# Two layers of a diffusion block and two of a second block on one core: column sums of the norms in sets of four tiles, and the scalings and biases around the norms on other engines

## The chip, the cores and the metric

One core of a Trainium2 chip runs the kernel. The metric is the time of one execution on the device in microseconds; three executions of the kernel before were timed. Engines are TensorE (PE, its weight loads PEld), VectorE (DVE), ScalarE (ACT), GpSimd (POOL) and SyncE (SP, which issues the DMAs).

## What is computed

The reference, cut to what matters here. All is float32, D is 1024, 512 latent tokens and, in layer 0, 256 context tokens.

```python
def layer_norm(t, g, b):
    tf = t.astype(jnp.float32)
    mu = jnp.mean(tf, axis=-1, keepdims=True)
    var = jnp.mean(jnp.square(tf - mu), axis=-1, keepdims=True)
    return ((tf - mu) * lax.rsqrt(var + LN_EPS)).astype(t.dtype) * g + b

def conformer_conv(u, dw_w, dw_b, ln_g, ln_b, pw_w, pw_b):
    a, gt = jnp.split(u, 2, axis=-1)
    h = depthwise_conv(a * jax.nn.sigmoid(gt), dw_w, dw_b)
    h = jax.nn.silu(layer_norm(h, ln_g, ln_b))
    return h @ pw_w + pw_b

def first_block(...):
    for l in range(DEPTH):
        ...
        attn_l = latent_attention(q_l, k_l, v_l, k_c, v_c)
        x = layer_norm(DEEPNORM_ALPHA * x + ml[..., 2, :] * mix(zl, attn_l), ln1_g[l], ln1_b[l])
        x = layer_norm(DEEPNORM_ALPHA * x + ml[..., 5, :] * ffn(modulate(x, ml[..., 3, :], ml[..., 4, :])),
                       ln2_g[l], ln2_b[l])
        ...
    return x

def second_block(x, p, positions, ...):
    h = x
    for i in range(DEPTH):
        u = rmsnorm(h, ln_mix[i]) @ w_in[i]
        ...
        h = h + jnp.concatenate([y_mla, y_gla], axis=-1) @ w_out[i]
        gate = jax.nn.sigmoid(rmsnorm(h, ple_norm[i]) @ w_ple_gate[i])
        h = h + gate * (p[i] @ w_ple_proj[i])
    return rmsnorm(h, final_norm)
```

`mix` adds three gated branches (attention, the conv branch above, a pooling branch) and multiplies by `w_out`. In layer 0 the context tokens go the same way with modulations of their own; in layer 1 only the latent tokens leave the block.

## The kernel before

Activations lie feature-major: a tensor of 1024 features is eight tiles of 128 partitions, with tokens along the free axis (768 in layer 0, 512 in layer 1 and in the second block). A product in float32 is three matmuls: operands are split into a high and a low part, and `proj` issues hi x hi, lo x hi and hi x lo. Weights come by DMA into `wr`; ScalarE casts the high part (`wh`, L178), VectorE subtracts the low one (`wl`, L181). All matmuls are issued from one line, L186.

A layer norm works on the eight tiles. `ln_center` (L231) adds the columns of each tile with a matmul against ones (`colsum`, L221): the sum of tile i goes to 32 columns of TensorE and 32 partitions of a PSUM tile `st`, column tile i % 4, so that tiles 0 and 4 share one. A matmul against `cmean` then adds the four parts and broadcasts, and VectorE subtracts the mean (L243). `inv_rms` (L246) squares each tile on ScalarE (L252) and issues that tile's sum right behind its square:

```python
        for i, y in enumerate(ys):
            sq = tmp()
            nc.scalar.activation(sq[:, :n], y, AF.Square)
            j = i % 4
            ...
                self.mm(s2[32 * j:32 * j + 32, c:c + w], self.ones[:, :32], sq[:, c:c + w], i < 4, i >= m - 4)
```

The reciprocal root is a chain of small VectorE steps (L209 to L214), and `ln_tile` broadcasts it over the partitions with identity matmuls. `ln_split` (L278) scales a tile on VectorE (L281), adds the bias and rounds to the high part on ScalarE (L282), and takes the low part on VectorE (L283); `split` does the last two for other tiles (L286, L287). In a chunk of over 512 tokens a sum is two matmuls.

A layer of the first block runs `mixer`, then `out_ffn`:
- at the end of `mixer` the conv norm: eight tiles reloaded from DRAM (L719), its sums between the projections of the gates, then for each tile scale (VectorE, L732), bias (GpSimd, L733), tanh (ScalarE, L735), product (VectorE, L736) and split; then the pointwise projection `conv_pw`, whose results are gated and added to the other branches (L750, L751) and split for `w_out`;
- in `out_ffn` the eight tiles of x are loaded (L778) and multiplied by ALPHA plus a bias on GpSimd (L780); the output projection adds into them on VectorE (L795); LN1 follows in two sections of tokens (512 and 256 in layer 0, 256 and 256 in layer 1), its scale copied to a tile `rs` (L800), `ln_split` gives the FFN's input, and GpSimd scales the raw tiles for the residual (L808, L809), with `ag` the gain and bias times ALPHA;
- the FFN adds into the same tiles (L831), and LN2's sums follow.

Between the layers `ln_split` makes layer 1's input from LN2, and GpSimd scales the tiles again (L1005, L1006) and stores them to DRAM tiles `xd`, which layer 1 loads as x. Behind layer 1 every second tile's bias is added on GpSimd (L1023). The second block's norms are RMS norms (`inv_rms` alone, tiles `pt`).

The order on each engine is set by a scheduler that simulates the program with a cost model, so the text of the program gives dependencies and a first order only. Each engine then runs its instructions in that fixed order.

Of the kernel before, what the change touches and what calls it, by code (L numbers as in the profile page):

```python
# [20 lines left out]
P = 128  # L21
D = 1024
KT = 8
# [54 lines left out]
class Net:  # L78
# [106 lines left out]
    def mm(self, out, l, r, start, stop):  # L185
        self.nc.tensor.matmul(out, l, r, start=start, stop=stop)  # L186
# [35 lines left out]
    def colsum(self, ps, tiles, n):  # L222

        m = len(tiles)
        for i, t in enumerate(tiles):
            j = i % 4
            for c in range(0, n, 512):
                w = min(512, n - c)
                self.mm(ps[32 * j:32 * j + 32, c:c + w], self.ones[:, :32], t[:, c:c + w], i < 4, i + 4 >= m)
# [15 lines left out]
    def inv_rms(self, ys, n, d, eps, tmp, out=None):  # L245
# [3 lines left out]
        m = len(ys)  # L249
        for i, y in enumerate(ys):  # L250
            sq = tmp()
            nc.scalar.activation(sq[:, :n], y, AF.Square)  # L252
            j = i % 4
            for c in range(0, n, 512):
                w = min(512, n - c)
                self.mm(s2[32 * j:32 * j + 32, c:c + w], self.ones[:, :32], sq[:, c:c + w], i < 4, i >= m - 4)
# [414 lines left out]
    def mixer(self, l, xsrc, hs, toks, region):  # L671
# [58 lines left out]
        for t in range(KT):  # L730
            y = ys[t]
            nc.vector.scalar_tensor_tensor(y[:, :n], y[:, :n], self.col(l, "cln_g")[:, t:t + 1], rb, ALU.mult, ALU.mult)  # L732
            nc.gpsimd.tensor_scalar(y[:, :n], y[:, :n], self.col(l, "cln_b")[:, t:t + 1], None, op0=ALU.add)  # L733
# [26 lines left out]
    def out_ffn(self, l, xsrc, mh):  # L760
# [14 lines left out]
        xs = []  # L775
        for t in range(KT):
            x = self.X()
            nc.sync.dma_start(x[:, :n], xsrc[t][:, :n])  # L778
            for s, (c0, sn) in enumerate(segs):
                nc.gpsimd.tensor_scalar(x[:, c0:c0 + sn], x[:, c0:c0 + sn], ALPHA, gb[:, t, s:s + 1], op0=ALU.mult, op1=ALU.add)  # L780
            xs.append(x)
# [4 lines left out]
        h2 = [(None, None)] * KT  # L786
        for s, (c0, sn) in enumerate(bsegs):
# [19 lines left out]
            for t in range(KT):  # L807
                nc.gpsimd.tensor_tensor(yv[t], yv[t], rs, ALU.mult)  # L808
                nc.gpsimd.tensor_scalar(yv[t], yv[t], ag[:, 0, t:t + 1], ag[:, 1, t:t + 1], op0=ALU.mult, op1=ALU.add)  # L809
# [5 lines left out]
        for nf in FCHS:  # L815
# [3 lines left out]
            if f0 == 0:  # L819
                gs += self.ffn_first(l, h2, bsegs, segs, n)  # L820
            gs += [self.ffn_up(l, f, h2, segs, n) for f in fs[len(gs):]]
# [54 lines left out]
    def block1(self, es1):  # L876
# [91 lines left out]
        with ExitStack() as es:  # L968
# [19 lines left out]
            for s, (c0, sn, r) in enumerate(rs):  # L988
                with tc.high_priority(offset=self.bprio if s == 0 else 0):
# [4 lines left out]
                    for t in range(KT):  # L994
# [7 lines left out]
                        self.ln_split(*h, xs[t][:, c0:c0 + sn], rb, G[:, t, s:s + 1], Bt[:, t, s:s + 1], self.B()[:, :sn])  # L1002
# [707 lines left out]
```

## Time and profile before

| | us |
|---|---|
| median of 3 executions | 3476.34 (3474.51 to 3477.19) |
| the profiled execution | 3477.77 |
| its span in the trace | 3476.0 |
| TensorE busy | 3252.7 (94%) |
| VectorE busy | 2215.7 (64%) |
| ScalarE busy | 1381.4 (40%) |
| GpSimd busy | 528.7 (15%) |

The mean granted clock of TensorE over the span is 0.961 of full speed. Shares are averages over stages with different limits; what a change of one stage is worth is read from the wait that ends last there. A row of a timeline gives start, length, engine, line and operation, result <- operands, shape and count, and in brackets the idle time just before it and what ended it. A group of instructions gives busy time and the mean of one in ns, and then the idle time of its engine just before them.

### The profile page before, as it was taken

Reading aid. Unit: us, or ns where it says so; the run is one execution under the profiler, and the core shown is the slowest. Engines: PE = TensorE matmul, PEld = TensorE weight load, DVE = VectorE, ACT = ScalarE, POOL = GpSimd, SP = SyncE. Lnnn points to the kernel's source line nnn. Section 1 sums busy time; section 2 is a strip of 40 time slices with the busy share of each in tenths; the row PEclk is TensorE's granted clock in tenths of the full one; section 3 lists DMA queues with packets and bytes.
Section 4 is the critical chain, followed back from the end, with each engine's and each line's share of the span. In section 5 each row is a group of like instructions: output and inputs, shape, how many; then the busy total and the mean of one; then the engine's idle time right before and its main releaser. Section 6 shows DMA issues by size and latency. Waiting matters only on the chain.

```text
span 3476.0 us, 47198 instructions
## 1 busy us (share of the span) xinstructions
PE 3252.7 (94%) x18622; PEld 2680.6 (77%) x18622; DVE 2215.7 (64%) x3623; ACT 1381.4 (40%) x2362; POOL 528.7 (15%) x581
## 2 busy tenths in 40 slices
PE   7999999899999999999999989999998979998897
PEld 4887787778778888877888857788877757886586
DVE  5795968744554444457988956654555675657655
ACT  2434343433332112233544434432335545554453
POOL 2120212222120000003111204200001220112101
PEclk8999999999999999998999999999999989999899
DMA  6232312233333432232222234433333222442223
GB/s 250 67 117 88 120 56 70 68 98 93 102 122 128 140 122 64 58 106 82 76 66 85 88 99 131 122 96 97 97 115 107 90 68 85 148 155 86 79 87 108
DMA packets 110909, 350.80 MB, mean 101 GB/s; under 512 B 12832, under 2 KB 19424, under 8 KB 105568
## 3 DMA queue, kind: packets, MB, share of 16 engines
q1 hardware_dynamic: 110688, 347.79, 31.5%
q8 instruction: 146, 2.39, 0.3%
q14 instruction: 75, 0.61, 0.1%
HBM read 326.77 MB, written 20.97 MB: 100 GB/s over the span
## 4 chain that ended last, share of the span: by engine, by line
PE 71%; DVE 13%; ACT 3%; issue 2%; POOL 1%; DMA 0%; POOLq 0%; DVEq 0%; SPq 0%; ACTq 0%
PE pp L186 59%; DVE W L593 5%; PE st L186 3%; PE ps L186 3%; PE pv L186 2%; DVE wl L181 1%; PE pt L186 1%; DVE T L287 1%; DVE s L489 1%; ACT wh L178 0%; DVE M L287 0%; PE pt L527 0%; PE gb L1457 0%; DVE s L212 0%; ACT M L286 0%
## 5 line engine op out<-in xcount | busy, mean ns | idle before, releaser
L181 DVE TENSOR_TENSOR wl<-wr,wh 128x1024 fp32r<-128x1024 f32 (+2 forms) x482 | 589.5, 1226 | 353.7 <-ACT wh L178 351.5
L178 ACT CAST wh<-wr 128x1024 fp32r<-128x1024 f32 (+2 forms) x482 | 490.8, 1021 | 768.8 <-PE pp L186 701.1
L186 PE MATMUL pp<-A,wh 128*128 128x512 f32 (+1 forms) x3392 | 774.6, 343 | 17.8 <-ACT A L286 7.9
L186 PE MATMUL pp<-C,wh 128*128 128x512 f32 (+1 forms) x2328 | 658.5, 368 | 31.6 <-DVE M L1212 18.5
L186 PEld LDWEIGHTS pp<-A,wh 128*128 128x128 f32 x3392 | 537.7, 191 | 128.7 <-issue 25.1
L186 PEld LDWEIGHTS pp<-C,wh 128*128 128x128 f32 x2328 | 415.8, 192 | 123.0 <-issue 35.1
L186 PE MATMUL pp<-A,wl 128*128 128x512 f32 (+1 forms) x1696 | 460.4, 340 | 0.0
L186 PE MATMUL pp<-C,wl 128*128 128x512 f32 (+1 forms) x1164 | 424.9, 366 | 0.0
L186 PE MATMUL pp<-B,wh 128*128 128x512 f32 (+1 forms) x1296 | 315.9, 350 | 0.0
L186 PE MATMUL pp<-M,wh 128*128 128x256 f32 (+1 forms) x1280 | 293.8, 324 | 12.9 <-ACT M L1114 4.5
L186 PEld LDWEIGHTS pp<-A,wl 128*128 128x128 f32 x1696 | 271.9, 190 | 39.4 <-issue 4.7
L593 DVE SCALAR_TENSOR_TENSOR W<-W,cw,W 128x783 f32<-128x783 f32 x240 | 269.2, 1125 | 2.1
L186 PEld LDWEIGHTS pp<-C,wl 128*128 128x128 f32 x1164 | 223.0, 192 | 44.2 <-issue 8.6
L186 PEld LDWEIGHTS pp<-M,wh 128*128 128x128 f32 x1280 | 214.6, 194 | 43.3 <-issue 14.1
L186 PEld LDWEIGHTS pp<-B,wh 128*128 128x128 f32 x1296 | 212.1, 188 | 37.8 <-issue 2.9
L186 PE MATMUL pp<-M,wl 128*128 128x256 f32 (+1 forms) x640 | 205.8, 322 | 0.0
L186 PE MATMUL pp<-B,wl 128*128 128x512 f32 (+1 forms) x648 | 193.5, 349 | 0.0
L593 DVE SCALAR_TENSOR_TENSOR W<-U,cw,W 128x512 f32<-128x512 f32 x240 | 189.2, 789 | 3.0
L866 DVE SCALAR_TENSOR_TENSOR B<-pp,cols,B 128x511 f32<-128x511 f32 x66 | 43.4, 658 | 211.6 <-ACT B L863 211.4
L831 DVE SCALAR_TENSOR_TENSOR X<-pp,g,X 128x512 f32<-128x512 f32 (+1 forms) x128 | 76.9, 630 | 156.2 <-PE pp L186 155.9
L863 ACT ACTIVATE B<-pp,cols 128x768 f32<-128x768 f32 (+1 forms) x44 | 38.9, 885 | 232.9 <-PE pp L186 232.9
L186 PEld LDWEIGHTS pp<-M,wl 128*128 128x128 f32 x640 | 124.3, 194 | 9.2 <-issue 2.0
(398 smaller groups left out, 4938.5 us busy)
## 6 DMA issues: line engine op xcount, KB each, us to landing
wr<-w_in SPq DMA_DIRECT2D x184, 512.0 KB, 3.8
wr<-w_up SPq DMA_DIRECT2D x96, 512.0 KB, 3.8
wa<-w_ada SPq DMA_DIRECT2D x40, 1024.0 KB, 5.0
wr<-w_out SPq DMA_DIRECT2D x64, 512.0 KB, 3.9
wr<-w_down SPq DMA_DIRECT2D x48, 512.0 KB, 3.6
wr<-w_ple_gate SPq DMA_DIRECT2D x32, 512.0 KB, 4.1
Z<-w_ada SPq DMA_DIRECT2D x16, 512.0 KB, 8.5
wr<-conv_pw SPq DMA_DIRECT2D x16, 512.0 KB, 3.8
```

The costliest lines, as they stand in the source:

```text
L178: nc.scalar.copy(hi[:, :n], raw[:, :n])
L181: eng.tensor_tensor(lo[:, :n], raw[:, :n], hi[:, :n].bitcast(F32), ALU.subtract)
L186: self.nc.tensor.matmul(out, l, r, start=start, stop=stop)
L287: self.nc.vector.tensor_tensor(lo, t, hi.bitcast(F32), ALU.subtract)
L489: nc.vector.tensor_reduce(nm, ps[:, :n], AX.X, ALU.max, negate=True)
L593: nc.vector.scalar_tensor_tensor(y, gl[:, i:i + no], ws[:, i:i + 1], y, ALU.mult, ALU.add)
L831: nc.vector.scalar_tensor_tensor(xs[t][:, c0:c0 + sn], ps[:, c0:c0 + sn], g5[:, t, q:q + 1], xs[t][:, c0:c0 + sn], ALU.mult, ALU.add)
L863: nc.scalar.activation(y[:, :n], pa[:, :n], AF.Identity, bias=self.col(l, "fdw_b")[:, f:f + 1], scale=cw[:, 1:2])
L866: nc.vector.scalar_tensor_tensor(y[:, c0 + 1:e], pa[:, c0:e - 1], cw[:, 0:1], y[:, c0 + 1:e], ALU.mult, ALU.add)
```

## The change

1. `colsum` takes the tiles four at a time and issues their matmuls next to each other, the last of the four first; `in_order` ties each to the one before without a semaphore. Given `square`, it squares four tiles first; `inv_rms` calls it so.
2. The conv norm's bias goes from GpSimd to ScalarE.
3. x times ALPHA plus a bias (L780) goes from GpSimd to ScalarE. LN2's scaling between the layers (L1005, L1006) is dropped: the raw tiles go to `xd`, the norm's factors to a DRAM tile `rld`, and layer 1 loads both (`rt`), scales on VectorE in one step, with the bias folded into `gb`.
4. The residual scaling behind LN1 becomes one step on VectorE and one on ScalarE, written behind the first FFN projections.
5. The last bias for even tiles goes from GpSimd to VectorE.

```diff
@@ -183,7 +183,7 @@
         return W(pieces, kp, mc)
     def mm(self, out, l, r, start, stop):
-        self.nc.tensor.matmul(out, l, r, start=start, stop=stop)
+        return self.nc.tensor.matmul(out, l, r, start=start, stop=stop)
     def proj(self, ps, w, m0, m1, xs, segs, ks=None, start=True, stop=True):
@@ -219,14 +219,29 @@
         for t in range(nt):
             self.mm(ps[:, t * P:(t + 1) * P], r[:, t:t + 1].broadcast_to([P, P]), self.ident, True, True)
-    def colsum(self, ps, tiles, n):
+    def in_order(self, ins):
+        for a, b in zip(ins, ins[1:]):
+            self.tc.add_manual_dep(b.ins, a.ins.name, mybir.DependencyInfo(mybir.DependencyClass.NoSync, mybir.DependencyReason.DATA),
+                                   reason="in_order")
+    def colsum(self, ps, tiles, n, square=None):
         m = len(tiles)
-        for i, t in enumerate(tiles):
-            j = i % 4
+        for i0 in range(0, m, 4):
+            fs = tiles[i0:i0 + 4]
+            if square is not None:
+                sq = [square() for _ in fs]
+                for o, t in zip(sq, fs):
+                    self.nc.scalar.activation(o[:, :n], t, AF.Square)
+                fs = sq
             for c in range(0, n, 512):
                 w = min(512, n - c)
-                self.mm(ps[32 * j:32 * j + 32, c:c + w], self.ones[:, :32], t[:, c:c + w], i < 4, i + 4 >= m)
+                ins = []
+                for j in [len(fs) - 1] + r_(0, len(fs) - 1):
+                    ins.append(self.mm(ps[32 * j:32 * j + 32, c:c + w], self.ones[:, :32], fs[j][:, c:c + w], i0 == 0, i0 + 4 >= m))
+                self.in_order(ins)
     def ln_center(self, ys, n, tmp):
@@ -246,14 +261,7 @@
         nc = self.nc
         s2 = self.ps("st")
-        m = len(ys)
-        for i, y in enumerate(ys):
-            sq = tmp()
-            nc.scalar.activation(sq[:, :n], y, AF.Square)
-            j = i % 4
-            for c in range(0, n, 512):
-                w = min(512, n - c)
-                self.mm(s2[32 * j:32 * j + 32, c:c + w], self.ones[:, :32], sq[:, c:c + w], i < 4, i >= m - 4)
+        self.colsum(s2, ys, n, tmp)
         cp = tmp()
         nc.scalar.copy(cp[:, :n], s2[:, :n])
         nt = n // P
@@ -730,7 +738,7 @@
         for t in range(KT):
             y = ys[t]
             nc.vector.scalar_tensor_tensor(y[:, :n], y[:, :n], self.col(l, "cln_g")[:, t:t + 1], rb, ALU.mult, ALU.mult)
-            nc.gpsimd.tensor_scalar(y[:, :n], y[:, :n], self.col(l, "cln_b")[:, t:t + 1], None, op0=ALU.add)
+            nc.scalar.activation(y[:, :n], y[:, :n], AF.Identity, bias=self.col(l, "cln_b")[:, t:t + 1])
             th = self.B()
             nc.scalar.activation(th[:, :n], y[:, :n], AF.Tanh, scale=0.5)
             nc.vector.scalar_tensor_tensor(th[:, :n], th[:, :n], 1.0, y[:, :n], ALU.add, ALU.mult)
@@ -757,7 +765,7 @@
                     mh.append((a, b))
         return mh
-    def out_ffn(self, l, xsrc, mh):
+    def out_ffn(self, l, xsrc, mh, norm=None):
         nc, tc = self.nc, self.tc
         last = l == DEPTH - 1
@@ -773,17 +781,29 @@
         gb = self.c1.tile([P, 8, 2], F32, tag="aff", bufs=8, name=self.nm("gb"))
         nc.vector.tensor_tensor(gb, self.mod(l, 2), self.col(l, "b_out").unsqueeze(2).broadcast_to([P, 8, 2]), ALU.mult)
         xs = []
+        if norm is not None:
+            rsd, g, b = norm
+            rt = self.B()[:, :n]
+            nc.sync.dma_start(rt, rsd)
+            an = self.c1.tile([P, 8], F32, name=self.nm("an"))
+            nc.vector.tensor_scalar(an, g, ALPHA, None, op0=ALU.mult)
+            nc.vector.scalar_tensor_tensor(gb, b.unsqueeze(2).broadcast_to([P, 8, 2]), ALPHA, gb, ALU.mult, ALU.add)
         for t in range(KT):
             x = self.X()
             nc.sync.dma_start(x[:, :n], xsrc[t][:, :n])
+            if norm is not None:
+                nc.vector.scalar_tensor_tensor(x[:, :n], x[:, :n], an[:, t:t + 1], rt, ALU.mult, ALU.mult)
             for s, (c0, sn) in enumerate(segs):
-                nc.gpsimd.tensor_scalar(x[:, c0:c0 + sn], x[:, c0:c0 + sn], ALPHA, gb[:, t, s:s + 1], op0=ALU.mult, op1=ALU.add)
+                nc.scalar.activation(x[:, c0:c0 + sn], x[:, c0:c0 + sn], AF.Identity, bias=gb[:, t, s:s + 1],
+                                     scale=1.0 if norm is not None else ALPHA)
             xs.append(x)
         G2, B2 = self.affine_mod(l, 4, 3, self.col(l, "ln1_g"), self.col(l, "ln1_b"))
         ag = self.c1.tile([P, 2, 8], F32, tag="ag", bufs=1, name=self.nm("ag"))
         nc.vector.tensor_scalar(ag[:, 0, :], self.col(l, "ln1_g"), ALPHA, None, op0=ALU.mult)
         nc.vector.tensor_scalar(ag[:, 1, :], self.col(l, "ln1_b"), ALPHA, None, op0=ALU.mult)
         h2 = [(None, None)] * KT
+        resid = []
         for s, (c0, sn) in enumerate(bsegs):
             q = gsel(c0)
             for pr in range(4):
@@ -804,9 +824,7 @@
                     h2[t] = (self.al("AB"[t // 4], F32R), self.al("AB"[t // 4], F32R))
                 a, b = h2[t]
                 self.ln_split(a[:, c0:c0 + sn], b[:, c0:c0 + sn], yv[t], rb, G2[:, t, q:q + 1], B2[:, t, q:q + 1], e[:, :sn])
-            for t in range(KT):
-                nc.gpsimd.tensor_tensor(yv[t], yv[t], rs, ALU.mult)
-                nc.gpsimd.tensor_scalar(yv[t], yv[t], ag[:, 0, t:t + 1], ag[:, 1, t:t + 1], op0=ALU.mult, op1=ALU.add)
+            resid.append((yv, rs))
         g5 = self.c1.tile([P, 8, 2], F32, tag="aff", bufs=8, name=self.nm("g5"))
         nc.vector.tensor_scalar(g5, self.mod(l, 5), 0.5, None, op0=ALU.mult)
         if not last:
@@ -818,6 +836,10 @@
             gs = []
             if f0 == 0:
                 gs += self.ffn_first(l, h2, bsegs, segs, n)
+                for yv, rv in resid:
+                    for t in range(KT):
+                        nc.vector.scalar_tensor_tensor(yv[t], yv[t], ag[:, 0, t:t + 1], rv, ALU.mult, ALU.mult)
+                        nc.scalar.activation(yv[t], yv[t], AF.Identity, bias=ag[:, 1, t:t + 1])
             gs += [self.ffn_up(l, f, h2, segs, n) for f in fs[len(gs):]]
             for sg in ([[s] for s in bsegs] if lastc else [segs]):
                 for pr in range(4):
@@ -1000,14 +1022,12 @@
                             h = (x[:, :256], x[:, 256:])
                             hc.append(h)
                         self.ln_split(*h, xs[t][:, c0:c0 + sn], rb, G[:, t, s:s + 1], Bt[:, t, s:s + 1], self.B()[:, :sn])
+            rld = self.dr.tile([P, SEQ], F32, name="rld")
+            nc.sync.dma_start(rld, rl)
             for t in range(KT):
-                yv = xs[t][:, :SEQ]
-                nc.gpsimd.tensor_tensor(yv, yv, rl, ALU.mult)
-                nc.gpsimd.tensor_scalar(yv, yv, self.col(0, "ln2_g")[:, t:t + 1], self.col(0, "ln2_b")[:, t:t + 1],
-                                        op0=ALU.mult, op1=ALU.add)
-                nc.sync.dma_start(xd[t], yv)
+                nc.sync.dma_start(xd[t], xs[t][:, :SEQ])
             mh = self.mixer(1, xd, hl, [(hl, 0), (hl, 256), (hc, 0)], region)
-            xs, rs = self.out_ffn(1, xd, mh)
+            xs, rs = self.out_ffn(1, xd, mh, (rld, self.col(0, "ln2_g"), self.col(0, "ln2_b")))
             closed()
             ps = opened(tc.tile_pool(name="P12", bufs=1, space=PSUM, reuse_waits="tile"))
             self.pstags = {"st": (ps, 2, 512)}
@@ -1020,7 +1040,7 @@
                         if t % 2:
                             nc.scalar.activation(xv, xv, AF.Identity, bias=b)
                         else:
-                            nc.gpsimd.tensor_scalar(xv, xv, b, None, op0=ALU.add)
+                            nc.vector.tensor_scalar(xv, xv, b, None, op0=ALU.add)
             closed()
         return xs
```

Counts by engine: TensorE keeps its 17845 matmuls; VectorE gets 50 more instructions, ScalarE 72, GpSimd 128 fewer, SP 2 more. The scheduler sets the order, so three places of it are shown. In the names, the part behind the last underline is the program's running number; line numbers are those of each kernel.

TensorE, layer 1, sums of the centre of the conv norm (`st`); `pp` are matmuls of a gate projection. Before:

```order
L186 MATMUL pp_17677<-C_13034,wh_17666 128x512
L186 MATMUL pp_17677<-C_13035,wh_17666 128x512
L186 MATMUL st_17525<-B_17509,ones 32x512
L186 MATMUL pp_17677<-C_13034,wl_17667 128x512
L186 MATMUL pp_17677<-C_13040,wh_17666 128x512
L186 MATMUL st_17525<-B_17511,ones 32x512
L186 MATMUL pp_17677<-C_13041,wh_17666 128x512
L186 MATMUL pp_17677<-C_13040,wl_17667 128x512
L186 MATMUL st_17525<-B_17513,ones 32x512
L186 MATMUL pp_17677<-C_13046,wh_17666 128x512
L186 MATMUL pp_17677<-C_13047,wh_17666 128x512
L186 MATMUL st_17525<-B_17515,ones 32x512
```

The change:

```order
L186 MATMUL pp_17663<-C_13065,wh_17658 128x512
L186 MATMUL pp_17663<-C_13064,wl_17659 128x512
L186 MATMUL st_17511<-B_17501,ones 32x512
L186 MATMUL st_17511<-B_17495,ones 32x512
L186 MATMUL st_17511<-B_17497,ones 32x512
L186 MATMUL st_17511<-B_17499,ones 32x512
L186 MATMUL pp_17663<-C_13070,wh_17658 128x512
L186 MATMUL pp_17663<-C_13071,wh_17658 128x512
L186 MATMUL pp_17663<-C_13070,wl_17659 128x512
L186 MATMUL pp_17663<-C_13076,wh_17658 128x512
L186 MATMUL pp_17663<-C_13077,wh_17658 128x512
```

Eight sums that each stood alone between filler matmuls become two sets of four.

VectorE, layer 0, LN1 of the latent tokens: `ln_split` (L281 and L283 before, L289 and L291 in the change), A and B its tiles, X the raw tiles. Before:

```order
L281 SCALAR_TENSOR_TENSOR B_8106<-X_7725,G_7741,st_8075 128x512
L283 SCALAR_TENSOR_TENSOR A_8084<-B_8082,Bt_7743,A_8083 128x512
L283 SCALAR_TENSOR_TENSOR A_8090<-B_8088,Bt_7743,A_8089 128x512
L283 SCALAR_TENSOR_TENSOR A_8096<-B_8094,Bt_7743,A_8095 128x512
L283 SCALAR_TENSOR_TENSOR A_8102<-B_8100,Bt_7743,A_8101 128x512
L283 SCALAR_TENSOR_TENSOR B_8108<-B_8106,Bt_7743,B_8107 128x512
L281 SCALAR_TENSOR_TENSOR B_8112<-X_7729,G_7741,st_8075 128x512
L283 SCALAR_TENSOR_TENSOR B_8114<-B_8112,Bt_7743,B_8113 128x512
```

The change:

```order
L289 SCALAR_TENSOR_TENSOR B_8106<-X_7725,G_7741,st_8075 128x512
L841 SCALAR_TENSOR_TENSOR X_7709<-X_7709,ag_7747,B_8080 128x512
L841 SCALAR_TENSOR_TENSOR X_7713<-X_7713,ag_7747,B_8080 128x512
L291 SCALAR_TENSOR_TENSOR A_8084<-B_8082,Bt_7743,A_8083 128x512
L841 SCALAR_TENSOR_TENSOR X_7717<-X_7717,ag_7747,B_8080 128x512
L291 SCALAR_TENSOR_TENSOR A_8090<-B_8088,Bt_7743,A_8089 128x512
L841 SCALAR_TENSOR_TENSOR X_7721<-X_7721,ag_7747,B_8080 128x512
L291 SCALAR_TENSOR_TENSOR A_8096<-B_8094,Bt_7743,A_8095 128x512
L841 SCALAR_TENSOR_TENSOR X_7725<-X_7725,ag_7747,B_8080 128x512
L291 SCALAR_TENSOR_TENSOR A_8102<-B_8100,Bt_7743,A_8101 128x512
```

The residual's scaling (L841) now stands between the scale and the low parts, though it is written behind the FFN's first projections.

VectorE, layer 1, where the output projection begins: `wl` low parts of its weights, C the split tiles, X the loaded x, B_18253 the factors loaded from `rld`. Before:

```order
L750 SCALAR_TENSOR_TENSOR B_18251<-B_17861,B_18251 128x512
L751 TENSOR_TENSOR X_17877<-X_17877,B_18251 128x512
L181 TENSOR_TENSOR wl_18430<-wr_18428,wh_18429 128x1024
L287 TENSOR_TENSOR C_18260<-X_17877,C_18259 128x512
L795 SCALAR_TENSOR_TENSOR X_18267<-pp_18312,g_18263,X_18267 128x256
```

The change:

```order
L796 SCALAR_TENSOR_TENSOR X_18278<-X_18278,an_18255,B_18253 128x512
L796 SCALAR_TENSOR_TENSOR X_18282<-X_18282,an_18255,B_18253 128x512
L181 TENSOR_TENSOR wl_18429<-wr_18427,wh_18428 128x1024
L295 TENSOR_TENSOR C_18246<-X_17863,C_18245 128x512
L181 TENSOR_TENSOR wl_18435<-wr_18433,wh_18434 128x1024
L815 SCALAR_TENSOR_TENSOR X_18258<-pp_18311,g_18249,X_18258 128x256
L815 SCALAR_TENSOR_TENSOR X_18262<-pp_18337,g_18249,X_18262 128x256
L796 SCALAR_TENSOR_TENSOR X_18286<-X_18286,an_18255,B_18253 128x512
```

Seven scalings of x (the first two rows are the last of them) now stand ahead of a weight split and of the last split tile that the output projection reads (L295, L287 before).

## Rows read from the trace of the kernel before

**Rows 1.** The page, part 1: busy time of each engine.

```profile
PE 3252.7 (94%) x18622; PEld 2680.6 (77%) x18622; DVE 2215.7 (64%) x3623; ACT 1381.4 (40%) x2362; POOL 528.7 (15%) x581
```

**Rows 2.** The page, part 4: the chain that ended last.

```profile
PE 71%; DVE 13%; ACT 3%; issue 2%; POOL 1%; DMA 0%; POOLq 0%; DVEq 0%; SPq 0%; ACTq 0%
```

**Rows 3.** Windows: stretch, length, busy us (instructions) per engine, PEclk, DMA share, GB/s.

```profile
699.00:738.00 39.00, 38.33 (x181) 23.79 (x182) 11.99 (x12) 8.71 (x11) 4.42 (x2) 1.00 0.38 129
...
1560.00:1600.00 40.00, 31.05 (x154) 25.18 (x154) 28.66 (x52) 12.75 (x29) 27.01 (x32) 0.60 0.24 86
2040.00:2080.00 40.00, 40.00 (x128) 19.10 (x127) 8.37 (x11) 10.91 (x18) 0.00 (x0) 1.00 0.24 79
```

**Rows 4.** Groups by line and shape, PE: all column sums of the norms.

```profile
L186 PE MATMUL st<-B,ones 128*32 128x512 f32 x96 | 37.3, 604 | 1.4 <-DVE X L664 1.4
...
L186 PE MATMUL st<-B,ones 128*32 128x256 f32 x128 | 30.0, 448 | 8.5 <-DVE X L243 4.1 <-DVE s L212 3.3 <-ACT B L252 1.1
...
L186 PE MATMUL pt<-C,ones 128*32 128x256 f32 x160 | 26.4, 414 | 4.6 <-ACT C L252 4.6
...
L186 PE MATMUL st<-X,ones 128*32 128x256 f32 x96 | 9.9, 387 | 0.0
...
L186 PE MATMUL st<-X,ones 128*32 128x512 f32 x32 | 5.9, 600 | 0.0
```

**Rows 5.** Timeline, PE: layer 1, conv norm, centre sums (start, length, operation).

```profile
2040.95 1.04 PE L186 MATMUL st<-B,ones 128*32 128x512 f32 x2
2041.93 0.50 PE L186 MATMUL pp<-C,wl 128*128 128x512 f32 x1
2042.27 0.40 PE L186 MATMUL pp<-C,wh 128*128 128x512 f32 x1
2042.59 1.05 PE L186 MATMUL st<-B,ones 128*32 128x512 f32 x2
```

**Rows 6.** Timeline, PE: layer 1, LN1, one sum of 256 tokens.

```profile
2225.20 0.62 PE L186 MATMUL st<-B,ones 128*32 128x256 f32 x2
...
2225.75 0.51 PE L186 MATMUL pp<-B,wh 128*128 128x256 f32 x2
```

**Rows 7.** Timeline, PE: layer 0, conv norm, one sum of 768 tokens.

```profile
699.67 1.48 PE L186 MATMUL st<-B,ones 128*32 128x512 f32 x4 [1.43 <-DVE X L664]
701.08 0.96 PE L186 MATMUL pp<-A,wh 128*128 128x512 f32 x4
```

**Rows 8.** Timeline, PE: layer 0, LN1, centre sums of seven tiles in a row.

```profile
906.51 1.92 PE L186 MATMUL st<-X,ones 128*32 128x512 f32 x14
```

**Rows 9.** Timeline, PE: layer 1, conv norm, filler at full clock; end of the wait.

```profile
2088.25 0.40 PE L186 MATMUL pp<-C,wl 128*128 128x512 f32 x1
...
2088.49 0.63 PE L186 MATMUL pp<-C,wh 128*128 128x512 f32 x2
...
2100.62 2.50 PE L186 MATMUL pp<-C,wh 128*128 128x512 f32 x5 [6.17 <-ACT C L286]
```

**Rows 10.** Waits of PE, 905 to 985 us: total, times, longest.

```profile
PE pp L186 <- ACT A L282: 4.5, 2, 2.9
```

**Rows 11.** Waits of PE, 1527 to 1600 us.

```profile
PE pp L186 <- ACT C L282: 4.5, 8, 0.6
```

**Rows 12.** Groups by line and shape, POOL.

```profile
L733 POOL TENSOR_SCALAR B<-B,cols 128x512 f32<-128x512 f32 x8 | 17.3, 2180 | 61.7 <-DVE B L732 61.7
...
L780 POOL TENSOR_SCALAR X<-X,gb 128x512 f32<-128x512 f32 x16 | 15.0, 939 | 49.0 <-DMA X<-xT 33.2 <-DMA X<-xd 9.7 <-DVE wl L181 4.2
```

**Rows 13.** Groups by line and shape, ACT.

```profile
L282 ACT ACTIVATE C<-C,Bt 128x512 fp32r<-128x512 f32 x8 | 5.8, 722 | 16.7 <-DVE C L281 16.7
...
L735 ACT ACTIVATE B<-B 128x512 f32<-128x512 f32 x8 | 5.0, 629 | 4.9 <-POOL B L733 4.9
```

**Rows 14.** Groups by line and shape, DVE.

```profile
L287 DVE TENSOR_TENSOR C<-B,C 128x512 fp32r<-128x512 f32 x26 | 17.6, 684 | 0.2
...
L283 DVE SCALAR_TENSOR_TENSOR C<-C,Bt,C 128x512 fp32r<-128x512 f32 x8 | 9.8, 1230 | 6.3 <-ACT C L282 6.3
```

## The prediction

> **What bounds the kernel now.** I read the page's busy shares first: TensorE is busy for 3252.7 of 3476.0 us, 94%, and GpSimd for 15% [rows 1]. Then the chain that ended last: 71% of it is TensorE, 13% VectorE, 1% GpSimd [rows 2]. So a microsecond of TensorE time is worth close to a microsecond, and one of GpSimd is worth something only where the chain of a norm runs through it. Third the stretches: while the conv norms add their columns TensorE is full (38.33 of 39 us in layer 0, 40.00 of 40 in layer 1), because projections fill the time around each sum, but at the start of layer 1 it is busy for 31.05 of 40 us at a granted clock of 0.60 [rows 3]: there the norm's chain sets the pace. Last the groups of the column sums: 37.3 + 30.0 + 26.4 + 9.9 + 5.9 = 109.5 us of TensorE time [rows 4], some 3% of the span, for matmuls that use 32 of 128 columns.
>
> **Part 1, the sums of four tiles side by side.** One sum over 512 tokens that stands alone holds TensorE from 2040.95 to 2041.93, 0.98 us [rows 5]; over 256 tokens 0.55 [rows 6]; over 768 1.41 [rows 7]. Where seven tiles stand next to each other in the program, their 14 records (a sum is two) end after 1.92 us [rows 8]: a set of four and one of three, so at most 0.96 a set. Four sums to four column tiles cost what one costs, and the price is the number of sets, not of sums.
>
> I counted sets in the two orders of TensorE and multiplied. Conv norm of layer 0: centre 8 sets become 2, at 1.41 (8.5 us saved), squares 5 become 2 (4.2). Conv norm of layer 1: 8 and 7 sets become 2 each, at 0.98 (5.9 and 4.9). The 512-token norms of layer 0 (LN1 and LN2, centre 3 to 2, squares 4 to 2): 6 sets, 5.9. The 256-token norms of layer 1, at 0.55: LN1 3 to 2, 7 to 2, 4 to 2 and 8 to 2, LN2 4 to 2 and 8 to 2: 22 sets, 12.1. The second block: 6 to 3 twice, 4 to 2 twice, 7 to 2: 15 sets, 8.3. The others already stand as eight in a row. Sum: 49.8 us.
>
> Each run of sums also costs its neighbours. Beside a lone sum the two filler matmuls start 0.34 and 0.32 us before what follows them [rows 5], against 0.24 in undisturbed filler [rows 9]: 0.18 a run. By the orders 104 runs become 50, so 54 x 0.18 = 9.7 us at most; shorter neighbours may lose less, and I take 8. Term: **-58 us**, bounds -50 and -60.
>
> The squares now wait for four ScalarE results where one did. This costs nothing while filler runs; where the squares pace TensorE, the last set still starts with the last square, as before. What does not come through is time saved just ahead of a wait for a chain that has not become shorter. I take **+5**, bounds 0 and +14 (a quarter of the term).
>
> The Trainium skill, page "TensorE: Matmul & The Clock Gate", Part 3, "Measured speedup vs the span model", gives 2.38 times for three column tiles and 3.07 times for four row tiles, so a set would cost about 1.3 of one sum. By that page's figures the term would be smaller by some 15 us, as an estimate. The trace here does not agree, with 1.92 us for a set of four and one of three [rows 8], and the sum goes by it.
>
> **Part 2, the conv norm's bias from GpSimd to ScalarE.** In layer 1 TensorE waits 6.17 us for the first split tile, and the five matmuls behind take 2.50 us instead of five times 0.24 [rows 9]. GpSimd's step is 2.18 us a tile [rows 12], ScalarE's work on such a tile 0.63 [rows 13]. One step lies ahead of the first tile and some of the next ones ahead of the rest: 1.55 us at least, and all 6.17 + 1.3 at most. Eight more filler matmuls also fall into the wait by the new order (1.9 us). I take **-5**. In layer 0 the same move puts eight Identities next to eight tanhs, splits and weight casts on ScalarE, some 28 us of work in a window of 25, in place of a GpSimd that ran beside it. The wait there was 2.3 us; I take **+1**, bounds -2 and +4.
>
> **Part 3, the scaling of x.** GpSimd waited 49.0 us ahead of these steps, 42.9 of them for loads of x [rows 12]. Those waits now stand on ScalarE, and the weight casts for the output projection are queued behind them. Each is near 3 us when it comes, and the casts run some 10 us ahead of TensorE, so most of it is covered: **+1**, bounds 0 and +6. In layer 1 the new order has seven VectorE scalings, all needing one more load (the norm's factors, behind weight loads in SP's queue), ahead of a weight split and of the last split tile of the output projection. At 0.69 us, from the nearest VectorE form with two SBUF operands [rows 14], seven are 4.8 us; TensorE had no wait there. **+4**, bounds 0 and +10.
>
> **Part 4, the residual behind LN1.** Written later, but both orders place it in the chain of the split tiles that TensorE waits for: in LN1 of layer 0 it waited 4.5 us for two results of it [rows 10]. By the order one or two scalings come ahead of each VectorE split; at 0.69, two to four of them lie ahead of the tile that TensorE next needs: 1.4 to 2.8 us for each of four chains, and as much again on ScalarE where it is full. Against it, the splits no longer share time with GpSimd. I take +2 for layer 0 and +4 for layer 1: **+6**, bounds -3 and +14.
>
> **Part 5, LN2 into layer 1.** TensorE waits eight times 0.6 us for this chain [rows 11]. Its VectorE step lasts 1.23 us beside GpSimd's two steps, where one with as many operands lasts 0.68 [rows 14]. Take 0.55 off each of eight tiles and the 0.6 us waits nearly go; I take **-3**, bounds 0 and -5. The factors' store and the rest of the loads go beside it: 0. The last bias, eight VectorE steps of 256 tokens, changes engines within a chain: 0, bounds -2 and +2.
>
> Sum: -58 + 5 - 5 + 1 + 1 + 4 + 6 - 3 = -49. The profiled execution took 3477.8 us, 1.4 above the median of the runs shown, so 3476.3 - 49 = **3427 us**.
>
> **Rivals.**
> 1. The norms' chains take it back. Centre and squares of the conv norms lie ahead of a tile chain; if VectorE, ScalarE and the reloaded tiles do not get earlier, TensorE stands where it worked. The waits at the end of both chains speak for it; against it, no wait stands between sums and broadcast, and GpSimd leaves that chain. Lost are 23.5 us of sets and 19 runs x 0.18, 27 us in all: **3454 us**.
> 2. ScalarE becomes what TensorE waits for, and the kernel gets slower. It gains 72 operations, 52 us at 0.72 [rows 13], and inherits 49.0 us of waits [rows 12]. If all 101 us lay on the path through the weight casts and the split tiles, the time would be 3476.3 - 58 - 3 + 101 = **3516 us**; from about two thirds of it on the kernel is slower than before. For it: each engine works in a fixed order, so a waiting step holds all behind it. Against it: ScalarE is busy 40% [rows 1], and the stretches of the loads have the casts ahead.
> 3. The four tiles do not run fully side by side in the new order (last tile, then first, second, third), which no row of before shows. The sets left cost about 50 us (by my count of sets some 100 before, less 49.8). The bounds are nothing more [rows 8] and a whole sum more for each set, 50 us, if the last tile ran by itself ahead of the others; a third of that is 17 us: **3444 us**. Against it: seven tiles in a row also go from a last column tile to a first one, within 1.92 us. The Trainium skill's figures (part 1) would put it here.
> 4. The change does not do what it says, since the order is the scheduler's: fillers slip between the four sums, or gaps elsewhere use the gain up. Two norms of the second block do show 2 + 2 + 4. Taken over all norms it would leave the time at about **3470 us**.
>
> **How the numbers follow.** My forecast has 0.63, rival 1 0.16, rival 3 0.08, rival 4 0.06, rival 2 0.07. The bounds of the terms reach from -80 to -1, and not all go one way: for the forecast alone I take 20 us to either side. With rivals 1 and 3 inside, the range is **3407 to 3458 us**; rivals 2 and 4 and half of the tail are left out. A measurement can tell 0.2%, 7 us. Rivals 1 and 3 are faster too, and some of rival 4: faster 0.89, within it 0.05, slower 0.06.
>
> **What would show it.** The groups of ones matmuls should fall from 109.5 to about 60 us, with starts of four some ns apart. The wait at 2094 us should shrink to 1 to 3 us, the eight waits of 0.6 us should go, and TensorE's idle time (3476.0 - 3252.7 = 223 us) stay within 15 us. I would be wrong if TensorE's busy time falls by 50 us and its idle time rises by 30 (rivals 1 and 2: the first with waits in the conv norms, the second with waits for casts or for split tiles behind ScalarE), or if a set of four lasts 1.3 us.

## The result and the profile after

| | before | the change |
|---|---|---|
| median of 4 executions, us | 3475.43 (3467.44 to 3477.19) | 3431.84 (3431.28 to 3438.09) |
| ratio, 95% interval | | 0.9883 (0.9864 to 0.9902) |
| profiled execution, us | 3477.77 | 3431.91 |

The change is faster by 1.2%, 41 us (34 to 47); 3427 was forecast, in a range of 3407 to 3458. Later runs on other chips gave medians of 3466 to 3472 for the kernel before, so kernels are compared by their ratios to it on one chip; the change run again gave 0.9899 (0.9884 to 0.9914).

The page after, parts 1 and 4, to be read against [rows 1, 2]:

```profile
PE 3196.7 (93%) x18622; PEld 2661.8 (78%) x18622; DVE 2220.9 (65%) x3673; ACT 1422.8 (41%) x2434; POOL 387.0 (11%) x453
...
PE 69%; DVE 13%; ACT 3%; issue 2%; DMA 1%; POOL 1%; SPq 0%; POOLq 0%; DVEq 0%; ACTq 0%
```

TensorE's busy time falls by 56.0 us, its idle time rises from 223.3 to 233.4 (3430.1 - 3196.7). The bound is the same engine. The groups of column sums of the change, against [rows 4]:

```profile
L186 PE MATMUL pt<-C,ones 128*32 128x256 f32 x160 | 15.8, 440 | 7.0 <-ACT C L237 6.7
L186 PE MATMUL st<-B,ones 128*32 128x512 f32 x96 | 12.8, 604 | 0.3 <-ACT B L237 0.3
L186 PE MATMUL st<-B,ones 128*32 128x256 f32 x128 | 12.4, 474 | 11.3 <-ACT B L237 7.3 <-DVE X L258 4.1
...
L186 PE MATMUL st<-X,ones 128*32 128x256 f32 x96 | 7.5, 390 | 1.3 <-DVE X L853 0.6 <-DVE s L272 0.5 <-DVE X L815 0.3
L186 PE MATMUL st<-X,ones 128*32 128x512 f32 x32 | 4.3, 604 | 0.0
```

As many instructions, 52.8 us instead of 109.5. The idle time ahead of them has grown: where a chain feeds the sums, TensorE now stands for it. In layer 1's conv norm the eight centre sums read so (timeline of TensorE, against [rows 5]):

```profile
2033.72 1.06 PE L186 MATMUL st<-B,ones 128*32 128x512 f32 x8
2034.72 0.73 PE L186 MATMUL pp<-C,wh 128*128 128x512 f32 x2
...
2036.77 1.07 PE L186 MATMUL st<-B,ones 128*32 128x512 f32 x8
```

Eight records, four sums, hold TensorE for 1.00 us where one sum held it for 0.98.

**Stage by stage.** I matched the two traces by counting TensorE's matmuls without the column sums: both have 18086 in nearly the same order, so the start of the k-th, in one and the other, shows how far the change is ahead. The steps in us (minus is gained), with the runs that the text comes to. Run 11, the change once more on another chip, gives the same steps within 1.4 us, so one entry under that tells little by itself:

| stage (time in the trace before) | change | sums alone (run 1) | moves alone (run 2) | change, small tile moved back (run 5) | sums alone, layer 1's tiles at byte 64 (run 10) |
|---|---|---|---|---|---|
| start to conv norm, layer 0 (0 to 690) | -0.2 | -1.0 | 0.4 | -0.8 | -4.5 |
| conv norm, layer 0 (to 800) | -13.1 | -14.2 | -1.9 | -14.0 | -15.6 |
| pointwise and output projection (to 905) | 1.0 | 0.0 | 1.0 | 0.0 | 0.0 |
| LN1, layer 0 (to 985) | -0.7 | -2.5 | 2.5 | -0.6 | -1.4 |
| FFN, layer 0 (to 1527) | 8.5 | 0.0 | 8.1 | 0.0 | 0.0 |
| LN2 into layer 1 (to 1600) | -4.4 | -1.4 | -2.3 | -3.5 | -2.1 |
| layer 1 to its conv norm (to 2040) | -2.2 | -1.4 | -3.7 | 0.4 | -4.1 |
| conv norm, layer 1 (to 2110) | -11.1 | -9.8 | 1.7 | -9.9 | -11.2 |
| output projection, layer 1 (to 2171) | -1.2 | -0.4 | -1.0 | -0.4 | -1.4 |
| LN1, layer 1 (to 2250) | -3.0 | -4.8 | 7.4 | -3.1 | -4.1 |
| FFN, layer 1 (to 2570) | -1.7 | -0.1 | -1.9 | 0.0 | -9.5 |
| LN2 and start of the second block (to 2645) | -4.5 | -4.6 | 2.1 | -3.4 | -4.9 |
| second block (to the end) | -13.5 | -5.1 | -6.5 | -13.4 | -16.0 |

One row was in no term of the forecast: 8.5 us are lost in layer 0's FFN, which the change leaves as it was but for the residual's scaling at its start.

### The profile page after: what moved, and what is told of

Its sections match the earlier page's. It is cut to its first block, busy times and chain, and to the rows that moved or that the text cites. A ratio compares the mean times of both kernels' runs of the same rounds, so it can differ in the third digit from the quotient of the medians.

```text
span 3430.1 us, 47151 instructions
## 1 busy us (share of the span) xinstructions
PE 3196.7 (93%) x18622; PEld 2661.8 (78%) x18622; DVE 2220.9 (65%) x3673; ACT 1422.8 (41%) x2434; POOL 387.0 (11%) x453
## 4 chain that ended last, share of the span: by engine, by line
PE 69%; DVE 13%; ACT 3%; issue 2%; DMA 1%; POOL 1%; SPq 0%; POOLq 0%; DVEq 0%; ACTq 0%
PE pp L186 60%; DVE W L601 4%; PE ps L186 3%; PE st L186 2%; PE pv L186 2%; DVE wl L181 1%; ACT wh L178 1%; DVE T L295 1%; PE pt L186 1%; DVE s L497 0%; PE pt L535 0%; DMA C<-gmd 0%; DVE s L212 0%; PE gb L1477 0%; DVE M L1232 0%
## 5 line engine op out<-in xcount | busy, mean ns | idle before, releaser
L186 PEld LDWEIGHTS pp<-M,wh 128*128 128x128 f32 x1280 | 214.5, 194 | 38.9 <-issue 12.8
```

The costliest lines, as they stand in the source:

```text
L186: return self.nc.tensor.matmul(out, l, r, start=start, stop=stop)
```

## The experiments

The theory after the result: the sums carry the gain; the moves cost about what they bring; and the FFN's 8.5 us come from something that the change does by the way. The rivals stand with each run.

**1. The sums alone.** The kernel before with the new `colsum`, `in_order` and `inv_rms`; all scalings and biases as before.

```diff
-    def colsum(self, ps, tiles, n):
...
+    def in_order(self, ins):
...
+    def colsum(self, ps, tiles, n, square=None):
...
+        self.colsum(s2, ys, n, tmp)
```

> The kernel before with the sums in sets of four alone. Theory (the sums carry the gain, the prediction's -58 and +5): 53 us less, 3422 us, ratio 0.985, with TensorE's steps ahead by some 13 us behind the sums of layer 0's conv norm, 14 us in layer 1's, 10 to 14 us in the second block. Rival (the moves off GpSimd carry a good part of the 44 us measured): 15 us less or fewer, 3460 us or more.

Measured: 3432.49 us, ratio 0.9882 (0.9861 to 0.9902). The sums give all that the change gives, 41 us, but not the 53 that the terms had. By the table they give what was expected in layer 0's conv norm (14.2 us, 13 expected), and less in layer 1's (9.8 of 14) and in the second block (5.1 of 10 to 14).

**2. The moves alone.** The change with the old `colsum` and `inv_rms`.

```diff
-        self.colsum(s2, ys, n, tmp)
+        m = len(ys)
+        for i, y in enumerate(ys):
+            sq = tmp()
+            nc.scalar.activation(sq[:, :n], y, AF.Square)
...
```

> The change without the sums in sets of four: only the scalings and biases on their new engines. Theory (my terms for the moves, with the signs that the trace shows: layer 1's conv norm 3 us worse, LN2 into layer 1 3 us better, the rest near 0): 3475 us within 7, ratio 0.998 to 1.002. Rival (the moves bring a gain of their own): 3460 us or less. Rival (the moves cost and the sums hide it): 3485 us or more.

Measured: 3485.87 us, ratio 1.0046 (1.0031 to 1.0061), 16 us slower than before. The third expectation holds: the moves cost. The two traces are only 6.2 us apart: the FFN of layer 0 loses 8.1 us again and LN1 9.9 (2.5 and 7.4), while the second block gains 6.5, of which 5.0 lie where the granted clock was 1.00 against 0.89 before (3290 to 3353 us of the trace before). The two parts of the change do not add: up to 3200 us the moves, with what comes by the way, cost 13.2 us by themselves, and 5.9 beside the sums in sets (41.1 us ahead in run 1, 35.2 in the change). Most of that difference is LN1 of layer 1 (7.4 against 1.8 us); why was not tried.

**3. The conv norm's bias back on GpSimd.**

```diff
-            nc.scalar.activation(y[:, :n], y[:, :n], AF.Identity, bias=self.col(l, "cln_b")[:, t:t + 1])
+            nc.gpsimd.tensor_scalar(y[:, :n], y[:, :n], self.col(l, "cln_b")[:, t:t + 1], None, op0=ALU.add)
```

> The change with the conv norm's bias back on GpSimd. Theory (in layer 1 ScalarE's fixed order, four biases and a weight cast ahead of the first tanh, makes TensorE's wait of 7.7 us): the wait falls to 3 to 6 us, the time to about 3428 us. Rival (the wait is there because TensorE comes earlier and the chain of a tile is as long with GpSimd's 2.18 us): the wait stays at 7 us or more, 3432 us.

Measured: 3432.35 us, ratio 0.9892 (0.9876 to 0.9907); no difference that can be told. The wait did fall, and came back in pieces. The timeline of TensorE and ScalarE in the change, then in this run:

```profile
2066.11 1.06 PE L186 MATMUL st<-ident,s 128*128 128x128 f32 x8
...
2068.90 2.55 ACT L741 ACTIVATE B<-B,cols 128x512 f32<-128x512 f32 x4
2071.36 1.03 ACT L178 CAST wh<-wr 128x1024 fp32r<-128x1024 f32 x1
2072.29 0.68 ACT L570 ACTIVATE B<-pp,hb 128x512 f32<-128x512 f32 x1
2072.87 1.66 ACT L743 ACTIVATE B<-B 128x512 f32<-128x512 f32 x3
...
2078.57 2.50 PE L186 MATMUL pp<-C,wh 128*128 128x512 f32 x5 [7.69 <-ACT C L294]
```

```profile
2070.40 1.05 PE L186 MATMUL st<-ident,s 128*128 128x128 f32 x8
...
2080.43 2.50 PE L186 MATMUL pp<-C,wh 128*128 128x512 f32 x5 [5.25 <-ACT C L294]
...
2084.18 1.22 PE L186 MATMUL pp<-C,wh 128*128 128x512 f32 x2 [0.83 <-ACT C L294]
```

The broadcast before, to be read with [rows 9]:

```profile
2091.53 1.05 PE L186 MATMUL st<-ident,s 128*128 128x128 f32 x8
```

From the broadcast to the first split tile it is 12.5 us in the change, 10.0 with GpSimd, 9.1 before (2091.53 to 2100.62). In the change ScalarE does four biases, a weight cast and the tanh of a gate (L570) ahead of the conv norm's first tanh, as its order has it. With GpSimd the first tile is earlier, but TensorE then waits for the next ones. In both orders each step is done for several tiles before the next step begins; that this sets the end is argued, since no run took the tiles one by one.

**4. The residual behind LN1 back on GpSimd**, where it was in the program.

```diff
-            resid.append((yv, rs))
+            for t in range(KT):
+                nc.gpsimd.tensor_tensor(yv[t], yv[t], rs, ALU.mult)
+                nc.gpsimd.tensor_scalar(yv[t], yv[t], ag[:, 0, t:t + 1], ag[:, 1, t:t + 1], op0=ALU.mult, op1=ALU.add)
```

> The change with the residual behind LN1 back on GpSimd. Theory (the prediction's +6 us for that move): 3426 us, with LN1's waits shorter than in the change. Rival (the move is free, as the aligned traces of layer 0 show): 3432 us within 3, GpSimd's steps beside VectorE's splits lengthen these again to over 1 us.

Measured: 3429.97 us, ratio 0.9881 (0.9865 to 0.9897): within the uncertainty of both expectations. The traces tell more: LN1 is 1.9 us shorter in layer 0 and 3.4 in layer 1 than in the change. At the end of LN2 (2645 us) this run is 6.3 us ahead of the change, and the second block, which the edit does not touch, takes it back. TensorE's waits in LN1 of layer 0, in the change (890 to 972 us) and in this run (888 to 970):

```profile
PE pp L186 <- ACT A L290: 4.5, 2, 2.9
...
PE pp L186 <- DVE A L291: 3.5, 2, 3.1
```

```profile
PE pp L186 <- ACT A L290: 4.5, 2, 2.9
...
PE pp L186 <- DVE A L291: 1.3, 1, 1.3
```

The wait for VectorE's low part, 3.5 against 1.3 us, is what the residual's scaling ahead of it costs in layer 0.

**5 to 7. The 8.5 us of the FFN.** Both FFNs keep TensorE full; the windows of the two kernels (1300 to 1350 us in layer 0, 2380 to 2430 in layer 1; columns as in [rows 3]), before and then the change:

```profile
1300.00:1350.00 50.00, 50.00 (x291) 44.02 (x290) 22.27 (x27) 14.07 (x15) 0.00 (x0) 1.00 0.21 64
2380.00:2430.00 50.00, 50.00 (x215) 40.19 (x214) 24.05 (x28) 12.84 (x16) 0.00 (x0) 1.00 0.34 105
```

```profile
1300.00:1350.00 50.00, 50.00 (x285) 43.43 (x284) 21.90 (x27) 13.18 (x15) 0.00 (x0) 1.00 0.21 64
2380.00:2430.00 50.00, 50.00 (x216) 40.26 (x215) 25.14 (x30) 14.45 (x17) 0.00 (x0) 1.00 0.29 85
```

In layer 0, 285 matmuls in the time of 291, with the same granted clock of 1.00 and no wait. From start to start, a matmul of 512 tokens takes 234.7 ns (mean over 1000 to 1500 us, of those whose next start follows within 300 ns) instead of 229.5, and so it does, within 0.2 ns, in runs 2 to 4, on another chip; in the run of the sums alone it takes 229.6. So it is the kernel, not the chip. What these kernels share is the new tile `an` of 32 bytes a partition. By the built programs' allocation it lies ahead of all activations of the first block but the raw tiles X and moves them: from byte 97120 (96 beyond a multiple of 128) to 97152 (0 beyond one). Experiment 5 takes `an` from a ring that exists, 6 makes it 96 bytes wide, 7 puts the whole scaling of x back.

```diff
-            an = self.c1.tile([P, 8], F32, name=self.nm("an"))
+            an = self.c1.tile([P, 8, 2], F32, tag="aff", bufs=8, name=self.nm("an"))[:, :, 0]
```

```diff
-            an = self.c1.tile([P, 8], F32, name=self.nm("an"))
+            an = self.c1.tile([P, 24], F32, name=self.nm("an"))[:, :8]
```

```diff
...
-                nc.scalar.activation(x[:, c0:c0 + sn], x[:, c0:c0 + sn], AF.Identity, bias=gb[:, t, s:s + 1],
-                                     scale=1.0 if norm is not None else ALPHA)
+                nc.gpsimd.tensor_scalar(x[:, c0:c0 + sn], x[:, c0:c0 + sn], ALPHA, gb[:, t, s:s + 1], op0=ALU.mult, op1=ALU.add)
...
-            xs, rs = self.out_ffn(1, xd, mh, (rld, self.col(0, "ln2_g"), self.col(0, "ln2_b")))
+            xs, rs = self.out_ffn(1, xd, mh)
```

> The change with its new 32-byte tile (the gains times ALPHA) taken from a ring that already exists, so that all tiles behind it lie where they lay before. Theory (the 32 bytes move the activations of the first block from byte 96 to byte 0 of 128, and TensorE's matmuls of 512 tokens take 234.7 instead of 229.4 ns in layer 0): 229 to 230 ns again in layer 0's FFN, 234 in layer 1, 8 to 12 us less than the change, 3421 us. Rival (the pace differs for another reason, from chip to chip or with the order): 234 ns in layer 0, 3432 us.

> The change with that tile 96 bytes wide, which puts the activations of the first block at byte 64 of 128, where those of the second block lie (there 228 to 230 ns in each kernel). Theory (the byte within 128 sets the pace): 228 to 230 ns in layer 0 and in layer 1, 15 us or more below the change, 3415 us. Rival (layer 1's pace of 233 to 234 ns has another reason, its layout apart): 229 ns in layer 0 only, 3421 us; or 234 in both, 3432 us.

> The change with the scaling of x as before: on GpSimd, the scaled tiles stored between the layers, no new tile. Theory (of this move, only the 32 bytes cost; against it LN2 into layer 1 loses its 2.7 us): 229 to 230 ns in layer 0's FFN, 6 to 9 us less than the change, 3424 us, with the eight waits of 0.6 us back at the start of layer 1. Rival (ScalarE's and VectorE's waits for x cost by themselves, the prediction's +5): another 5 us less, 3419 us.

Measured: 5, 3428.49 us, ratio 0.9882 (0.9867 to 0.9897); 6, 3416.73, 0.9850 (0.9832 to 0.9868); 7, 3426.53, 0.9877 (0.9859 to 0.9895). The same windows in 5 and in 6:

```profile
1300.00:1350.00 50.00, 50.00 (x290) 44.03 (x289) 22.27 (x27) 14.06 (x15) 0.00 (x0) 1.00 0.21 66
2380.00:2430.00 50.00, 50.00 (x216) 40.18 (x215) 25.87 (x30) 14.98 (x18) 0.00 (x0) 1.00 0.32 99
```

```profile
1300.00:1350.00 50.00, 50.00 (x290) 44.06 (x290) 22.28 (x27) 14.07 (x16) 0.00 (x0) 1.00 0.20 65
2380.00:2430.00 50.00, 50.00 (x223) 41.40 (x222) 26.01 (x31) 17.24 (x21) 0.00 (x0) 1.00 0.28 88
```

The theory of the 32 bytes holds: with `an` elsewhere the FFN of layer 0 is as fast as before, 8.5 us in the aligned traces. Layer 1 then gives some of it back (its tiles at byte 96: 234.3 ns, at byte 0: 233.3), so the whole kernel gains 2.5 us in the trace, too little for the ratio to show. With byte 64 (run 6), layer 1's FFN takes 226.7 ns and gains 9.5 us; in layer 0 the expectation of 228 to 230 ns fails, with 232.4 ns and 1.8 us lost. Run 7 shows that the scaling of x as such costs nothing that can be told (from the pointwise projection to the output projection both layers take as long as in 5) and that the start of layer 1 loses 2.5 us with it on GpSimd (-1.0 against -3.5).

**8 to 11. Each layer at its best byte, and on one chip.** 8 is 5 with a pad of 96 bytes ahead of layer 1's tiles; 9 is 8 with the residual on GpSimd (as 4) and the conv norm's bias on VectorE; 10 is 1 with the pad; 11 is the change once more.

```diff
             cp = es.enter_context(tc.tile_pool(name="cp", bufs=1, reuse_waits="tile"))
+            pad = cp.tile([P, 24], F32, name="pad")
+            nc.gpsimd.memset(pad, 0.0)
```

```diff
-            nc.scalar.activation(y[:, :n], y[:, :n], AF.Identity, bias=self.col(l, "cln_b")[:, t:t + 1])
+            nc.vector.tensor_scalar(y[:, :n], y[:, :n], self.col(l, "cln_b")[:, t:t + 1], None, op0=ALU.add)
```

> The change with the activations at byte 96 of 128 in layer 0 (the small tile from an existing ring) and at byte 64 in layer 1 (a pad of 96 bytes ahead of that layer's tiles). Theory (each layer's pace goes with the byte at which its tiles lie): 229.4 ns in layer 0, 226 to 229 ns in layer 1, some 8 us less than the change in layer 0's FFN and 10 less in layer 1, 3413 us. Rival (the two do not add, or the later granted clock gives it back): 3422 us or more.

> The run before (both layers' bytes) with the residual behind LN1 on GpSimd and the conv norm's bias on VectorE instead of ScalarE. Theory (the residual costs 3 us a layer where it stands in the split tiles' chain; the bias on VectorE takes ScalarE's four biases out of the way of the first tanh): 5 to 8 us less than the run before, 3407 us, and the wait of layer 1's conv norm at 6 us or less. Rival (VectorE's chain becomes as long as ScalarE's was): the wait stays at 7 to 9 us, 3 us less by the residual alone.

> The kernel before with the sums in sets of four and layer 1's activations at byte 64; all scalings and biases on GpSimd as before. Theory (the moves bring only LN2's 3 us): within 5 us of the first run of this group plus 0 to 3, 3414 us. Rival (the moves are worth something with both bytes right): 3422 us.

> The change once more, on the chip of these runs, for a comparison on one chip: ratio 0.986 to 0.990 as before, layer 0's FFN at 234 to 235 ns.

Measured on one chip: 8, 3413.47 us, ratio 0.9841 (0.9827 to 0.9856); 9, 3415.60, 0.9851 (0.9831 to 0.9870); 10, **3404.48**, 0.9822 (0.9803 to 0.9841); 11, 3432.44, 0.9899 (0.9884 to 0.9914).

The bytes are worth 19 us to the change (8 against 11). Run 9 missed: no gain against 8. The traces show the residual's part (LN1 is 1.2 us shorter in layer 0, 1.1 in layer 1), but the wait in layer 1's conv norm became 9.4 us, which is the rival named there: VectorE's scales and biases of several tiles go ahead of the first product.

```profile
PE pp L186 <- ACT C L294: 9.4, 1, 9.4
```

Run 10, the sums in sets and the pad with every scaling left on GpSimd, beats both kernels, 62 us (55 to 68) under the kernel before; its lead of 9 us over run 8 is within the two intervals, which share the spread of the kernel before, but on the one chip its four executions (3402.90 to 3409.86) all lie under the four of run 8 (3411.09 to 3413.71). By the traces it is 7.6 us ahead at 2800 us. From 2850 to 2943 us, in work that neither edit touches, it gains 6.6 more at a granted clock of 1.00 against 0.89, and run 8 takes back 4 behind that. So with the bytes of both layers the same, the moves still cost some 7 us.

## Why the prediction was right, point by point

- **The sums.** Their price was right: a set of four costs 1.00 us, and the groups fell by 56.7 us (forecast: to about 60, measured 52.8). What came through was less than -58 + 5: the sums alone are 41 us by the ratio (34 to 48), 45 by the aligned trace. The term for time saved just ahead of a wait was the mis-sized one, +5 where 13 (trace) to 17 (ratio) would have been right; 3.6 of the 13 are the second block's pace, told of below. In layer 1's conv norm the run of the sums alone has gained 12.8 us when its sums are done and 9.8 behind the wait, so the chain took 3 us; LN1 of layer 1 gave 4.8 where its 14 sets and 13 runs had 10.0 (14 x 0.55 + 13 x 0.18).
- **The conv norm's bias.** The term of -5 in layer 1 failed. The wait grew from 6.17 [rows 9] to 7.69 us, since I counted ScalarE's 0.63 us against GpSimd's 2.18 [rows 12, 13] and left out ScalarE's order: it goes through several tiles, with casts between them, and the operation takes 0.71 us there. With the bias on ScalarE the wait was 7.7 to 8.9 us (the change, runs 2 and 4), on GpSimd 6.1 and 7.0 in two pieces (runs 3 and 1). At the same byte the stage gains 9.9 us with the move (run 5) and 9.8 without it (run 1): the move brought nothing. In layer 0 the move cost at most the 1 us that was forecast (-13.1 against -14.2 us in run 1; -14.5 in run 11).
- **The scaling of x.** +1 and +4 were forecast, and neither came. The 1.0 us lost in layer 0 belongs to the 32 bytes: run 5 has the scaling on ScalarE too and loses 0.0. In layer 1 nothing was lost (-1.2, and -0.4 in run 5). ScalarE waited 8.8 us for loads where GpSimd had waited 42.9: the scheduler put the operations later. The row of the scaling, in the change:

```profile
L798 ACT ACTIVATE X<-X,gb 128x512 f32<-128x512 f32 x16 | 10.9, 720 | 9.2 <-DMA X<-xT 8.8 <-DVE X L796 0.4
```

- **The residual.** +6 forecast; 5.3 measured by run 4 (1.9 + 3.4), 2.3 by run 9 against run 8 (1.2 + 1.1, beside the other move).
- **LN2 into layer 1.** -3 forecast, -2.6 measured from 1560 to 1600 us: 3.7 gained over the eight tiles, 1.1 lost in a longer wait ahead of them. The mechanism was as said, its sign in the waits not: VectorE's step fell from 1.23 us [rows 14] to 0.75, a tile's turn from 2.55 to 2.20 us, but the eight waits stayed, at 0.5 us a tile. With GpSimd's steps back (run 7) VectorE's step is 1.23 us again, and the move is worth 2.5 us (-1.0 against -3.5). The Trainium skill, page "SBUF — State Buffer", section "Who interferes with whom", says that a VectorE instruction with two inputs in SBUF contends with a GpSimd instruction that reads SBUF; the trace agrees, with 0.75 us where GpSimd's steps are gone and 1.23 where they stood beside it.

```profile
L291 DVE SCALAR_TENSOR_TENSOR C<-C,Bt,C 128x512 fp32r<-128x512 f32 x8 | 6.0, 751 | 6.3 <-ACT C L290 6.3
...
PE pp L186 <- ACT C L290: 4.0, 8, 0.6
```

- **The last bias.** 0 forecast; the stage that holds it gains 4.5 us in the change and 4.6 with the sums alone.
- **Left out.** The 32 bytes: +8.5 us in layer 0, and -1.7 in layer 1's FFN. It was in no term and no rival. With the 1.0 us named above, layer 0 lost 9.5 by it. Set against it, the second block gave 13.5 where 10.6 had been counted (15 sets, 13 runs). Of that, 3.9 us come between 3200 and 3353 us, where the same code takes longer the lower the granted clock: there the change and run 5 are 3.6 to 3.9 us ahead of the kernel before, run 1 is 2.6 behind. The same 294 matmuls (3290 to 3353 us before) took 63.0 us at a mean clock of 0.89 in the kernel before, 61.7 at 0.92 in the change, 66.5 at 0.82 in run 1 and 58.0 at 1.00 in run 2. For one piece of it the windows of the change and of run 6 read so (columns as in [rows 3]):

```profile
3275.00:3290.00 15.00, 14.17 (x60) 9.55 (x60) 8.53 (x21) 9.04 (x18) 0.00 (x0) 0.83 0.00 1
...
3264.00:3282.00 18.00, 17.68 (x57) 12.23 (x57) 8.35 (x21) 9.04 (x18) 0.00 (x0) 0.56 0.00 1
```

  No term had this clock either, and no run tried what sets it. So the total of 45.9 us in the trace came close to the forecast of 49 in part by luck: errors of both signs are in it.
- **The rivals.** Rival 1 (chains take the time back) is in part true: 3 us in one conv norm, not 27. Rival 2 (ScalarE holds all up) shows in one place, with the wait of 7.69 us. Rival 3 is out: 1.00 us a set. Rival 4 did not come: the order kept the sets.

## What to carry to other kernels

Sums into narrow column tiles are worth issuing side by side: count sets, then ask of each place whether filler or a chain follows. Moving small steps off a slow engine that runs beside the bound bought nothing here but in LN2 into layer 1; each engine works in a fixed order, and in layer 1's conv norm the shorter step left the longer wait (7.69 us, against 6.1 in two pieces). And when a stage that an edit does not touch changes its pace, compare the addresses of the two programs before looking for a cause in the edit.

## What the runs showed of the hardware

TensorE's pace for one and the same matmul (512 tokens, granted clock 1.00, no wait) went with the byte at which the activations lie in a partition, in each run that had it: in layer 0, 229.5 to 229.9 ns at byte 96 beyond a multiple of 128, 234.7 to 234.9 at byte 0, and 231 to 234 at byte 64 (run 6); in layer 1, 234 at 96, 233.3 at 0, and 226.7 to 229 at 64. The same byte is best in one layer and worst in the other, so the byte alone is not the rule. The layers differ in the width of a tile (3072 and 2048 bytes) and in what follows a matmul (mostly one of 256 tokens in layer 0, one of 512 in layer 1). The traces tell the two apart, since some 150 matmuls of 512 in layer 0's LN1 and FFN (960 to 1527 us) are followed by another of 512. In the tiles of 3072 bytes these take 234.0 ns at byte 96, 233.4 at 0 and 227.1 at 64, near layer 1's 234.3, 233.3 and 226.7; those followed by one of 256 take 229.4, 234.7 and 232.6 (kernel before, change, run 6). So the pace goes with the byte and with the matmuls that follow each other, and not with the width of the tile. Why, and whether it is TensorE's reads or its neighbours' accesses, was not tried and stays open.
